# A broadcast row kept in PSUM, its biases added on ScalarE, and the split of the weights' low parts, in the opening stage of a hybrid layer

## The chip, the cores and the metric

The kernel runs on one core of a Trainium2 chip. The metric is the device time of one execution in microseconds (us). A core has five engines with queues of their own, each in order: PE (TensorE: matmuls and transposes, results into PSUM), DVE (VectorE), ACT (ScalarE), POOL (GpSimd) and SP (SyncE, which issues the DMAs here). Engines meet only at semaphores.

## The reference

One layer, a batch of 1, 256 tokens, width 2048, all in float32. Only the head of it concerns the change:

```python
shift, scale, gate = jnp.split(jax.nn.silu(c) @ w_ada + b_ada, 3, axis=-1)
h = rms_norm(x, norm_pre_w) * (1.0 + scale[:, None]) + shift[:, None]
proj = h @ w_in
```

`c` is one vector of 2048, `w_ada` is 2048 x 6144, `w_in` 2048 x 24,656. Two recurrent branches (a gated DeltaNet with 32 heads, an mLSTM with 8) use the columns of `proj`, and are merged with `sigmoid` gates that are columns of `proj` too; two projections, `w_out`, a second norm and the residual follow.

## The kernel before

**Precision.** Every float32 matmul with weights is made of three passes in the faster format fp32r. A matrix is split in a high part (ACT casts it, `whi`) and a low part (the matrix less the high part, `wlo`), on DVE or on POOL. `mm3` (lines 215 to 217) then issues high x high, high x low and low x high into one PSUM bank. `split_w` (line 176) decides for each half tile of 128x1024 where the low part is made: `share` counts up by `START_SHARE` for each half, and when it reaches one, POOL makes it. In the opening stage 0.625 of the halves go to POOL, later none.

**The opening stage** computes h and, as h comes into being, 14 groups of 512 columns of `w_in` that need no recurrence (the merge gates and the gates of three pairs of mLSTM heads). h needs shift and scale, so 32 MB of `w_ada` have to be read first; to keep PE at work the stage goes by blocks of k, chunks of 128 of the 2048 input channels: (0, 2), (2, 2), (4, 4), (8, 4), (12, 4) (first chunk, count). In each block all 14 groups are multiplied for the block's chunks. Groups 2 to 13 leave a partial sum in SBUF after each block: in the first ACT copies it (line 398), later DVE adds the bank to it (line 400). Groups 0 and 1 stay in four PSUM banks (`pr`, from the pool `pg`) throughout, with no copies or additions. Groups 2 to 13 take turns in the other four banks (`pn`, pool `pj`).

**Shift and scale** are not made on PE. `csil`, the row silu(c) repeated on all 128 partitions of SBUF, is made once by POOL (`partition_broadcast`, line 266). An ada tile is 128 output channels x 2048 inputs (1 MB); DVE multiplies it by `csil` and sums along the row in one instruction (line 331). Tile 2k gives shift of chunk k, tile 2k+1 its scale. Line 340 adds the bias to shift; line 315, in `h_chunk`, makes the factor of the norm from scale; ACT then computes the chunk of h (line 318) and casts it, and POOL makes its low part `h_lo`. `h_chunk(k)` is called straight behind the product of tile 2k+1.

**The head.** x is loaded, squared and summed (lines 276, 277), and POOL takes the root (`rsx`, line 213). ACT scales x with it (line 285), PE transposes it (line 291), ACT copies it back (line 293).

**Order.** `Stream` keeps a list of units (one weight tile or one ada tile), prepares each some three pieces ahead of its use, and loads a tile when its place in a ring of three is free (one ring for `w_in`, one for ada; the row `c` takes a place in the latter). All these loads are in SP's one queue in the list's order. `PACE` says how many ada tiles stand in the list before each block. `side` holds generators that advance by one step at each use: here, near the end of the stage, the gates' small work (lines 423 to 488) from the columns `pab`, which are multiplied between blocks 3 and 4. `branches_open` ends the stage: it drops the stage's SBUF and opens that of the recurrence.

Of the kernel before, what the change touches and what calls it, by code (L numbers as in the profile page):

```python
# [7 lines left out]
F32 = mybir.dt.float32  # L8
F32R = mybir.dt.float32r
AF = mybir.ActivationFunctionType  # L10
ALU = mybir.AluOpType
# [4 lines left out]
P = 128  # L16
# [5 lines left out]
QSCALE = 128.0 ** -0.5  # L22


START_SHARE = 0.625
STEP_US = 2.1
ROOM_US = 2.5

# [88 lines left out]
def hybrid_layer_kernel(  # L117
# [30 lines left out]
    hp = ctx.enter_context(tc.tile_pool(name="hp", bufs=1))  # L148
    yp = ctx.enter_context(tc.tile_pool(name="yp", bufs=2))
    pj = ctx.enter_context(tc.tile_pool(name="pj", bufs=4, space=PSUM))  # L150
    pg = ctx.enter_context(tc.tile_pool(name="pg", bufs=4, space=PSUM))
    dr = ctx.enter_context(tc.tile_pool(name="dr", bufs=1, space=DRAM))

    def const(name, src, shape):
# [38 lines left out]
    def gtile(nm, held=False):  # L193
        i = slots[0] % 4
        slots[0] += 1
        t = pg.tile([P, 512], F32, name=nm, tag="g")
        freed[i] = 1 << 30 if held else side.t + 1
        slots[1][id(t)] = i, t
        return t
# [9 lines left out]
    def jtile(nm):  # L209
        return pj.tile([P, 512], F32, name=nm, tag="pj")  # L210
# [13 lines left out]
    sil = cp.tile([P, KC], F32, name="sil")  # L224
    A.activation(sil, ct, AF.Silu)
    con = cp.tile([P, 512], F32, name="con")
    ident = con[:, 0:128]
    bd32 = con[:, 128:256]
    eunit = con[:, 256:512].rearrange("p (q i) -> p q i", q=8)
# [21 lines left out]
    rs = sp.tile([P, 2], F32, name="rsx")  # L251
    ad = sp.tile([P, 32], F32, name="ad")
    s1 = sp.tile([P, KC], F32, name="s1")
    part = [None, None] + [sp.tile([P, 2, 512], F32, name=f"part{g}") for g in range(2, len(START))]
    ADA_BUFS = 3

    csil = sp.tile([P, D], F32, name="csil")
    crow = sp.tile([P, D], F32, name="crow", tag="ar", bufs=ADA_BUFS)[0:1]
    SP.dma_start(crow, c_row)
    for b in range(2):  # L260
# [2 lines left out]
    bat = const("bat", b_ada_t, [P, 32])  # L263
    npre = const("npre", npre_t, [P, KC])
    A.activation(crow, crow, AF.Silu)
    G.partition_broadcast(csil, crow)
    late_c = {}

    def late_consts():
# [25 lines left out]
    def x_chunks(k0, k1):  # L295

        x_scale(k0)
        for k in range(k0, k1, 2):
            if k + 2 < k1:
                x_scale(k + 2)  # L300
            x_turn(k)
# [10 lines left out]

    def h_chunk(k):

        V.scalar_tensor_tensor(s1[:, k:k + 1], ad[:, KC + k:KC + k + 1], npre[:, k:k + 1], bnp[:, k:k + 1],
                               op0=ALU.mult, op1=ALU.add)
        hf = sp.tile([P, S], F32, name="hf", tag="hf", bufs=2)
        A.activation(hf.rearrange("p (b t) -> p b t", b=2), xs[:, :, k * P:(k + 1) * P], AF.Identity, bias=ad[:, k:k + 1], scale=s1[:, k:k + 1])
        split(hf, h_hi[:, k], h_lo[:, k], G)

    stream = Stream(load_w, side)
    BLOCKS = ((0, 2), (2, 2), (4, 4), (8, 4), (12, 4))
    PACE = (4, 9.5, 16.5, 25, 32, 32)

    def ada_units():

        adders = []
        for k in range(KC):
            for pt in range(2):
                def prep(h, raw, k=k, pt=pt):  # L330
                    V.scalar_tensor_tensor(raw, raw, 1.0, csil, op0=ALU.mult, op1=ALU.mult,  # L331
                                           accum_out=ad[:, pt * KC + k:pt * KC + k + 1])
                    if 4 <= 2 * k + pt < 8:
                        j = 2 * (2 * k + pt)
                        if j > 8:
                            x_turn(j)
                        if j < 14:
                            x_scale(j + 2)
                    if pt == 0:
                        V.tensor_tensor(ad[:, k:k + 1], ad[:, k:k + 1], bat[:, k:k + 1], op=ALU.add)  # L340
                    else:
                        h_chunk(k)
                        if k == 0:
                            x_chunks(6, 10)
                    return ()
                adders.append(lambda i=2 * k + pt, prep=prep:
                              stream.add(w_ada[i], prep, None, 1, load=(load_ada, "ada", ADA_BUFS)))
        return adders

    resident = {}  # L350
    br = ExitStack()

    def branches_open():

        nonlocal bp, x0, y0
        side.drain()
        share[:] = [0.0, 0.0]
        st.close()
        bp = br.enter_context(tc.tile_pool(name="bp", bufs=2))

        x0 = bp.tile([P, 8, P], F32, name="x0", tag="x0", bufs=1)
        y0 = bp.tile([64, 8, 64], F32, name="y0", tag="y0", bufs=1)
        G.memset(x0, 0.0)
        G.memset(y0, 0.0)

    def add_start_groups(bi):
        k0, nk = BLOCKS[bi]
        lastb = bi == len(BLOCKS) - 1
        adders, parts_ = [], []
        for g in range(len(START)):  # L370
            st_ = {}

            def use(h, hi, lo, g=g, st_=st_):
                if h == 0:
                    if g < 2:
                        if bi == 0:
                            resident[g] = [gtile(f"pr{i}") for i in range(2)]
                        st_["ps"] = resident[g]
                    else:
                        st_["ps"] = [jtile(f"pn{i}") for i in range(2)]  # L380
                for kc in range(min(2, nk - 2 * h)):
                    kr = h * 2 + kc
                    k = k0 + kr
                    o = kc * 512
                    for b in range(2):
                        mm3(st_["ps"][b], h_hi[:, k, b * P:(b + 1) * P], h_lo[:, k, b * P:(b + 1) * P],
                            hi[:, o:o + 512], lo[:, o:o + 512],
                            kr == 0 if g >= 2 else k == 0, kr == nk - 1 if g >= 2 else k == KC - 1)

            def after(g=g, st_=st_):  # L390
                if g < 2 and lastb:
                    part[g] = sp.tile([P, 2, 512], F32, name="res", tag="ar", bufs=ADA_BUFS)
                for b in range(2):
                    if g < 2:
                        if lastb:
                            A.activation(part[g][:, b], st_["ps"][b], AF.Sigmoid)
                    elif bi == 0:
                        A.copy(part[g][:, b], st_["ps"][b])
                    else:
                        V.tensor_tensor(part[g][:, b], st_["ps"][b], part[g][:, b], op=ALU.add)  # L400
                if bi == len(BLOCKS) - 2 and g == 3:
                    late_consts()
                if lastb:
                    if g >= 2:
                        pt = part[g].rearrange("p b c -> p (b c)")
                        A.activation(pt, pt, AF.Silu if g in (9, 11, 13) else AF.Sigmoid)
                    if g < 8:
                        SP.dma_start(gate_dr[g], part[g])
                    elif g % 2:
                        V.tensor_tensor(part[g], part[g], part[g - 1], op=ALU.mult)  # L410
                        SP.dma_start(gate_dr[8 + (g - 8) // 2], part[g])
                    if g == NG - 1:
                        branches_open()
            parts_.append((w_in[START[g]][:, k0 * 512:(k0 + nk) * 512], use, after))
        if nk == 2:
            for g in range(0, NG, 2):
                def use2(h, hi, lo, g=g):
                    parts_[g + h][1](0, hi, lo)
                    parts_[g + h][2]()
                adders.append(lambda g=g, use2=use2:  # L420
                              stream.add((parts_[g][0], parts_[g + 1][0]), prep_w, use2))
        else:
            for src, use, after in parts_:
                adders.append(lambda src=src, use=use, after=after:
                              stream.add(src, lambda h, raw: prep_w(h, raw, nk * 512), use, (nk + 1) // 2, after))
        return adders
# [63 lines left out]
    def add_ab():  # L490
        st_ = {}

        def use(h, hi, lo):
            if h == 0:
                st_["ps"] = jtile("pab")
            for j in range(8):
                k = h * 8 + j
                mm3(st_["ps"][:, 0:S], hi[:, j * P:(j + 1) * P], lo[:, j * P:(j + 1) * P], h_hi[:, k], h_lo[:, k],
                    k == 0, k == KC - 1)
        stream.add(w_ab, prep_w, use, after=lambda: side.add(gates(st_["ps"])))  # L500
# [4 lines left out]
    for bi, (k0, nk) in enumerate(BLOCKS):  # L505
        if bi == len(BLOCKS) - 1:
            add_ab()
        fs = add_start_groups(bi)
        for j, f in enumerate(fs):
            due = PACE[bi] + (PACE[bi + 1] - PACE[bi]) * j / len(fs)  # L510
            while ia < len(ada) and ia < due:
                ada[ia]()
                ia += 1
            f()
# [795 lines left out]
```

## Time and profile before

| | us |
|---|---|
| median of 3 runs | 1675.74 (1673.32 to 1677.84) |
| the profiled execution | 1673.93 |
| its span, first to last instruction | 1672.0 |
| busy in the span: PE, DVE, ACT, POOL | 1598.9, 1215.2, 923.4, 306.5 |
| busy from 26 to 300: PE, DVE, ACT, POOL | 249.6, 227.5, 123.3, 180.4 |
| mean granted clock of PE | 0.994 of full speed |
| moved by DMA | 372.4 MB, mean 223 GB/s |

A row of the timeline gives the start, the duration, the engine, the line, the operation, output <- inputs, shapes and a count, and in brackets how long the engine stood idle before it and what ended that. A row of the groups gives busy time and mean ns, then the idle time ahead. A row of the waits gives who waited for whom: total, times, longest. Matmuls overlap, so the duration of one (0.39 us) is longer than the distance from one to the next; PE's busy time is no measure of full pace.

### The profile page before, as it was taken

The page shows a single profiled execution, that of the slowest core. Times are in us where ns is not written, and L with a number is a line of the kernel's source. Part 1 is how long each engine was busy: PE and PEld are TensorE (multiplying, and loading weights), DVE is VectorE, ACT ScalarE, POOL GpSimd, SP SyncE. Part 2 cuts the span into 40 slices and gives each one's busy share as a digit, 9 for nine tenths or more (in the row PEclk, how much of TensorE's full clock was granted, in tenths as well). Part 3 has the DMA queues.
Part 4 walks back from the last instruction along what each step waited for, and adds up shares of the span by engine and source line. Part 5 has one row for each costly group of instructions (what it writes and reads, how often), then busy time and mean ns, then how long its engine had stood idle before and what let it go on. Part 6 is the DMA issues. An engine that isn't in the chain of part 4 may idle for free.

```text
span 1672.0 us, 25381 instructions
## 1 busy us (share of the span) xinstructions
PE 1598.9 (96%) x9836; PEld 1397.9 (84%) x9836; DVE 1215.2 (73%) x1799; ACT 923.4 (55%) x1462; POOL 306.5 (18%) x201
## 2 busy tenths in 40 slices
PE   3889999999999999999999999999999999999997
PEld 2767787778999898989898989889889788888886
DVE  5788888665677778787878787876778556756654
ACT  4733343755555657575757565755654644444443
POOL 2656766552000000000000000000010000100101
PEclk9989999999999999999999999999999999999999
DMA  9776776666555555555555555557888668766572
GB/s 348 283 276 252 301 282 231 227 239 227 183 187 170 179 164 186 183 178 171 173 176 183 166 168 178 178 164 248 282 285 307 251 248 292 276 243 237 210 269 109
DMA packets 96259, 372.37 MB, mean 223 GB/s; under 512 B 26261, under 2 KB 46213, under 8 KB 58249
## 3 DMA queue, kind: packets, MB, share of 16 engines
q1 hardware_dynamic: 96138, 370.75, 63.1%
q8 instruction: 77, 1.26, 0.3%
q14 instruction: 44, 0.36, 0.1%
HBM read 354.40 MB, written 16.31 MB: 222 GB/s over the span
## 4 chain that ended last, share of the span: by engine, by line
PE 64%; issue 15%; DVE 10%; ACT 5%; POOL 3%; DMA 2%; SPq 0%; DVEq 0%; ACTq 0%; POOLq 0%
PE pt L217 24%; PE pn L217 22%; PE py L217 8%; DVE wlo L169 3%; DVE ar L331 3%; ACT whi L168 2%; POOL wlo L169 2%; PE pr L217 1%; DVE part L400 1%; POOL mg L1118 1%; PE psa L217 1%; DVE gacc L1017 1%; DMA ya<-o_dr 1%; PE mq L761 1%; PE mz L769 1%
## 5 line engine op out<-in xcount | busy, mean ns | idle before, releaser
L169 DVE TENSOR_TENSOR wlo<-raw,whi 128x1024 fp32r<-128x1024 f32 x441 | 577.9, 1318 | 274.1 <-ACT whi L168 270.2
L168 ACT CAST whi<-raw 128x1024 fp32r<-128x1024 f32 x514 | 528.8, 1051 | 264.2 <-PE pn L217 92.6
L217 PE MATMUL pt<-h_hi,whi 128*128 128x256 f32 x1280 | 368.2, 288 | 0.0
L217 PE MATMUL pt<-h_hi,wlo 128*128 128x256 f32 x1280 | 362.6, 283 | 2.4 <-DVE wlo L169 1.5
L217 PE MATMUL pt<-h_lo,whi 128*128 128x256 f32 x1280 | 362.0, 283 | 0.0
L217 PE MATMUL pn<-whi,h_hi 128*128 128x512 f32 x832 | 331.2, 398 | 17.9 <-DVE part L400 9.4
L217 PE MATMUL pn<-wlo,h_hi 128*128 128x512 f32 x832 | 327.2, 393 | 4.9 <-POOL wlo L169 3.0
L217 PE MATMUL pn<-whi,h_lo 128*128 128x512 f32 x832 | 326.4, 392 | 0.0
L217 PEld LDWEIGHTS pt<-h_hi,wlo 128*128 128x128 f32 x1280 | 245.1, 191 | 3.5 <-DVE wlo L169 2.4
L217 PEld LDWEIGHTS pt<-h_hi,whi 128*128 128x128 f32 x1280 | 245.2, 192 | 1.4
L217 PEld LDWEIGHTS pt<-h_lo,whi 128*128 128x128 f32 x1280 | 245.3, 192 | 0.2
L169 POOL TENSOR_TENSOR wlo<-raw,whi 128x1024 fp32r<-128x1024 f32 x73 | 210.7, 2904 | 67.1 <-ACT whi L168 64.2
L217 PEld LDWEIGHTS pn<-whi,h_hi 128*128 128x128 f32 x832 | 157.7, 190 | 56.3 <-issue 9.8
L217 PEld LDWEIGHTS pn<-wlo,h_hi 128*128 128x128 f32 x832 | 157.7, 190 | 39.8 <-POOL wlo L169 5.5
L217 PEld LDWEIGHTS pn<-whi,h_lo 128*128 128x128 f32 x832 | 157.5, 189 | 33.5
L217 PE MATMUL py<-whi,yhi 128*128 128x512 f32 x384 | 150.6, 392 | 0.5 <-ACT vt L948 0.5
L217 PE MATMUL py<-whi,ylo 128*128 128x512 f32 x384 | 149.6, 389 | 0.0
L217 PE MATMUL py<-wlo,yhi 128*128 128x512 f32 x384 | 149.5, 389 | 0.0
L587 POOL TENSOR_SCALAR_AFFINE_SELECT dd<-gb 128x256 f32<-128x256 f32 x40 | 20.6, 538 | 441.4 <-DMA gb<-rows 341.0
L331 DVE SCALAR_TENSOR_TENSOR ar<-ar,csil 128x2048 f32<-128x2048 f32 x32 | 97.2, 3036 | 2.9 <-DMA ar<-in_dram 2.9
L168 ACT CAST yhi<-ya 128x512 fp32r<-128x512 f32 x48 | 29.9, 622 | 125.3 <-PE py L217 123.4
L169 DVE TENSOR_TENSOR ylo<-ya,yhi 128x512 fp32r<-128x512 f32 x48 | 33.2, 692 | 90.4 <-ACT yhi L168 88.5
(249 smaller groups left out, 2002.8 us busy)
## 6 DMA issues: line engine op xcount, KB each, us to landing
raw<-in_dram SPq DMA_DIRECT2D x259, 1024.0 KB
ar<-in_dram SPq DMA_DIRECT2D x32, 1024.0 KB
raw<-in_dram SPq DMA_DIRECT2D x28, 512.0 KB
ya<-o_dr SPq DMA_DIRECT2D x32, 256.0 KB
gb<-rows SPq DMA_DIRECT2D x20, 256.0 KB
gate_dr<-part SPq DMA_DIRECT2D x9, 512.0 KB
ug<-ud SPq DMA_DIRECT2D x32, 128.0 KB
o_dr<-oT SPq DMA_DIRECT2D x16, 256.0 KB
```

What stands on the lines that cost most here:

```text
L168: A.copy(hi, src)
L169: (eng or V).tensor_tensor(lo, src, hi.bitcast(F32), op=ALU.subtract)
L217: T.matmul(ps, l, r, start=start and i == 0, stop=stop and i == 2, skip_group_check=True)
L331: V.scalar_tensor_tensor(raw, raw, 1.0, csil, op0=ALU.mult, op1=ALU.mult, accum_out=ad[:, pt * KC + k:pt * KC + k + 1])
L400: V.tensor_tensor(part[g][:, b], st_["ps"][b], part[g][:, b], op=ALU.add)
L587: G.affine_select(dd[:, :, blk * S:blk * S + P], gb[:, :, blk * P:(blk + 1) * P], pattern=[[0, 2], [1, P]], compare_op=ALU.is_ge, fill=-1e ...
L761: T.matmul(psp[64:128, m * 64:(m + 1) * 64], um(m)[0:64, 64:128], y0[:, m], start=True, stop=True)
L769: T.matmul(psz[0:64, m * 64:(m + 1) * 64], p2[64:128, m], x0[64:128, m, 64:128], start=True, stop=True)
L1017: V.scalar_tensor_tensor(gate_half[q], raw[:, q * 1024:(q + 1) * 1024], sil[:, i:i + 1], gate_half[q], op0=ALU.mult, op1=ALU.add)
L1118: G.tensor_tensor(mcols(b, hf, cg), mcols(b, hf, cg), s_, op=ALU.add)
```

## The change

1. `csil` is made by four matmuls of a row of ones with the row silu(c) and stays in four PSUM banks until the end of the stage; `partition_broadcast` goes. The pool `pg` opens only then.
2. So groups 0 and 1 aren't resident any more: all 14 groups are copied or added to a partial sum, block by block.
3. The bias of shift and the factor from scale are made on ACT (`sh` and `s1`, 128x1 each) and no longer on DVE.
4. A chunk of h isn't queued straight behind its product but at the next chunk's first ada tile, or when a matmul needs it (`due`, `h_chunks`); chunk 0 at once.
5. `START_SHARE` is 0.8, and it falls to 0 with the last ada tile, not at the end of the stage. One number of `PACE` is 26 for 25.

```diff
-START_SHARE = 0.625
+START_SHARE = 0.8
...
-    pg = ctx.enter_context(tc.tile_pool(name="pg", bufs=4, space=PSUM))
+    pg = None
...
+    one_row = cp.tile([1, P], F32, name="one_row")
+    V.memset(one_row, 1.0)
...
-    part = [None, None] + [sp.tile([P, 2, 512], F32, name=f"part{g}") for g in range(2, len(START))]
+    sh = sp.tile([P, KC], F32, name="sh")
+    part = [sp.tile([P, 2, 512], F32, name=f"part{g}") for g in range(len(START))]
...
-    csil = sp.tile([P, D], F32, name="csil")
+    pcs = ExitStack()
+    csil = pcs.enter_context(tc.tile_pool(name="pcs", bufs=1, space=PSUM)).tile([P, D], F32, name="csil")
...
-    G.partition_broadcast(csil, crow)
+    for q in range(4):
+        T.matmul(csil[:, q * 512:(q + 1) * 512], one_row, crow[:, q * 512:(q + 1) * 512], start=True, stop=True)
...
     def h_chunk(k):
-        V.scalar_tensor_tensor(s1[:, k:k + 1], ad[:, KC + k:KC + k + 1], npre[:, k:k + 1], bnp[:, k:k + 1],
-                               op0=ALU.mult, op1=ALU.add)
+        A.activation(sh[:, k:k + 1], ad[:, k:k + 1], AF.Identity, bias=bat[:, k:k + 1])
+        A.activation(s1[:, k:k + 1], ad[:, KC + k:KC + k + 1], AF.Identity, bias=bnp[:, k:k + 1],
+                     scale=npre[:, k:k + 1])
...
-    PACE = (4, 9.5, 16.5, 25, 32, 32)
+    PACE = (4, 9.5, 16.5, 26, 32, 32)
+    due = []
+    def h_chunks(k):
+        while due and due[0] <= k:
+            h_chunk(due.pop(0))
...
-                    if pt == 0:
-                        V.tensor_tensor(ad[:, k:k + 1], ad[:, k:k + 1], bat[:, k:k + 1], op=ALU.add)
-                    else:
-                        h_chunk(k)
+                    h_chunks(k - 1)
+                    if pt == 1:
+                        due.append(k)
                         if k == 0:
+                            h_chunks(0)
                             x_chunks(6, 10)
+                        elif k == KC - 1:
+                            share[1] = 0.0
...
     def branches_open():
-        share[:] = [0.0, 0.0]
         st.close()
+        pcs.close()
+        pg = ctx.enter_context(tc.tile_pool(name="pg", bufs=4, space=PSUM))
...
-                    if g < 2:
-                        if bi == 0:
-                            resident[g] = [gtile(f"pr{i}") for i in range(2)]
-                        st_["ps"] = resident[g]
-                    else:
-                        st_["ps"] = [jtile(f"pn{i}") for i in range(2)]
+                    st_["ps"] = [jtile(f"pn{i}") for i in range(2)]
...
                     k = k0 + kr
+                    h_chunks(k)
...
-                    if g < 2:
-                        if lastb:
-                            A.activation(part[g][:, b], st_["ps"][b], AF.Sigmoid)
-                    elif bi == 0:
+                    if bi == 0:
                         A.copy(part[g][:, b], st_["ps"][b])
```

What moves, at three places. First POOL, from the program's start on (after its constants); `ISA` rows have no tile of their own. Before:

```order
L266 ISA
L266 ISA csil<-crow 128x2048
L213 ISA
L213 TENSOR_TENSOR rsx<-rsx,mhalf 128x2
L169 TENSOR_TENSOR h_lo<-hf,h_hi 128x256 x2
L169 TENSOR_TENSOR wlo<-raw,whi 128x1024 x2
L169 TENSOR_TENSOR h_lo<-hf,h_hi 128x256
```

And now:

```order
L213 ISA
L213 TENSOR_TENSOR rsx<-rsx,mhalf 128x2
L169 TENSOR_TENSOR h_lo<-hf,h_hi 128x256
L169 TENSOR_TENSOR wlo<-raw,whi 128x1024
L169 TENSOR_TENSOR h_lo<-hf,h_hi 128x256
L169 TENSOR_TENSOR wlo<-raw,whi 128x1024 x3
L169 TENSOR_TENSOR h_lo<-hf,h_hi 128x256
```

The broadcast is gone from ahead of the root, the second chunk's low part stands behind the first of the weights', and more low parts follow between two chunks.

Second ACT, from the transposed x (`xs`) to the first copies of partial sums. Before:

```order
L293 COPY xs<-xps 128x2x256 x2
L318 ACTIVATE hf<-xs,ad,s_103 128x256
L168 CAST h_hi<-hf 128x256
L285 ACTIVATE xs<-xs,rsx 128x256 x4
L293 COPY xs<-xps 128x2x256 x2
L318 ACTIVATE hf<-xs,ad,s_103 128x256
L168 CAST h_hi<-hf 128x256
L168 CAST whi<-raw 128x1024 x2
```

And now:

```order
L299 COPY xs<-xps 128x2x256 x2
L321 ACTIVATE sh<-ad,bat 128x1
L322 ACTIVATE s_102<-ad,bnp,npre 128x1
L325 ACTIVATE hf<-xs,sh,s_102 128x256
L168 CAST h_hi<-hf 128x256
L291 ACTIVATE xs<-xs,rsx 128x256 x4
L299 COPY xs<-xps 128x2x256 x2
L168 CAST whi<-raw 128x1024 x2
L291 ACTIVATE xs<-xs,rsx 128x256 x2
L321 ACTIVATE sh<-ad,bat 128x1
L322 ACTIVATE s_102<-ad,bnp,npre 128x1
L325 ACTIVATE hf<-xs,sh,s_102 128x256
```

The first two casts of weights have come ahead of the second chunk of h, and each chunk brings two operations of one column.

Third DVE, at the start of block 1 (`part_104` is the first partial sum that is kept: group 2 before, group 0 now). Before:

```order
L331 SCALAR_TENSOR_TENSOR ar,ad<-ar,csil 128x2048
L340 TENSOR_TENSOR ad<-ad,bat 128x1
L400 TENSOR_TENSOR part_105<-pn_668,part_105 128x512
L400 TENSOR_TENSOR part_105<-pn_669,part_105 128x512
L169 TENSOR_TENSOR wlo<-raw,whi 128x1024
L400 TENSOR_TENSOR part_106<-pn_691,part_106 128x512
L400 TENSOR_TENSOR part_106<-pn_692,part_106 128x512
L331 SCALAR_TENSOR_TENSOR ar,ad<-ar,csil 128x2048
L315 SCALAR_TENSOR_TENSOR s_103<-ad,npre,bnp 128x1
```

And now:

```order
L344 SCALAR_TENSOR_TENSOR ar,ad<-ar,csil 128x2048
L405 TENSOR_TENSOR part_105<-pn_635,part_105 128x512
L405 TENSOR_TENSOR part_105<-pn_636,part_105 128x512
L405 TENSOR_TENSOR part_106<-pn_658,part_106 128x512
L405 TENSOR_TENSOR part_106<-pn_659,part_106 128x512
L344 SCALAR_TENSOR_TENSOR ar,ad<-ar,csil 128x2048
L169 TENSOR_TENSOR wlo<-raw,whi 128x1024
L405 TENSOR_TENSOR part_107<-pn_687,part_107 128x512
```

The column operations behind each product are gone, and a low part of weights stands between the additions less often.

More of the change, by code (lines that the diff above doesn't have):

```diff
@@ L313, in h_chunk @@
     def h_chunk(k):
-        V.scalar_tensor_tensor(s1[:, k:k + 1], ad[:, KC + k:KC + k + 1], npre[:, k:k + 1], bnp[:, k:k + 1],
-                               op0=ALU.mult, op1=ALU.add)
+        A.activation(sh[:, k:k + 1], ad[:, k:k + 1], AF.Identity, bias=bat[:, k:k + 1])
+        A.activation(s1[:, k:k + 1], ad[:, KC + k:KC + k + 1], AF.Identity, bias=bnp[:, k:k + 1],
+                     scale=npre[:, k:k + 1])
         hf = sp.tile([P, S], F32, name="hf", tag="hf", bufs=2)
-        A.activation(hf.rearrange("p (b t) -> p b t", b=2), xs[:, :, k * P:(k + 1) * P], AF.Identity, bias=ad[:, k:k + 1], scale=s1[:, k:k + 1])
+        A.activation(hf.rearrange("p (b t) -> p b t", b=2), xs[:, :, k * P:(k + 1) * P], AF.Identity, bias=sh[:, k:k + 1], scale=s1[:, k:k + 1])
         split(hf, h_hi[:, k], h_lo[:, k], G)
@@ L348, in ada_units @@
         return adders
-    resident = {}
     br = ExitStack()
     def branches_open():
-        nonlocal bp, x0, y0
+        nonlocal bp, pg, x0, y0
         side.drain()
-        share[:] = [0.0, 0.0]
         st.close()
+        pcs.close()
+        pg = ctx.enter_context(tc.tile_pool(name="pg", bufs=4, space=PSUM))
         bp = br.enter_context(tc.tile_pool(name="bp", bufs=2))
@@ L386, in use @@
                         mm3(st_["ps"][b], h_hi[:, k, b * P:(b + 1) * P], h_lo[:, k, b * P:(b + 1) * P],
-                            hi[:, o:o + 512], lo[:, o:o + 512],
-                            kr == 0 if g >= 2 else k == 0, kr == nk - 1 if g >= 2 else k == KC - 1)
+                            hi[:, o:o + 512], lo[:, o:o + 512], kr == 0, kr == nk - 1)
             def after(g=g, st_=st_):
-                if g < 2 and lastb:
-                    part[g] = sp.tile([P, 2, 512], F32, name="res", tag="ar", bufs=ADA_BUFS)
                 for b in range(2):
-                    if g < 2:
-                        if lastb:
-                            A.activation(part[g][:, b], st_["ps"][b], AF.Sigmoid)
-                    elif bi == 0:
+                    if bi == 0:
                         A.copy(part[g][:, b], st_["ps"][b])
@@ L403, in after @@
                 if lastb:
-                    if g >= 2:
-                        pt = part[g].rearrange("p b c -> p (b c)")
-                        A.activation(pt, pt, AF.Silu if g in (9, 11, 13) else AF.Sigmoid)
+                    pt = part[g].rearrange("p b c -> p (b c)")
+                    A.activation(pt, pt, AF.Silu if g in (9, 11, 13) else AF.Sigmoid)
                     if g < 8:
@@ L497, in use @@
                 k = h * 8 + j
+                h_chunks(k)
                 mm3(st_["ps"][:, 0:S], hi[:, j * P:(j + 1) * P], lo[:, j * P:(j + 1) * P], h_hi[:, k], h_lo[:, k],
@@ L509, in hybrid_layer_kernel @@
         for j, f in enumerate(fs):
-            due = PACE[bi] + (PACE[bi + 1] - PACE[bi]) * j / len(fs)
-            while ia < len(ada) and ia < due:
+            ahead = PACE[bi] + (PACE[bi + 1] - PACE[bi]) * j / len(fs)
+            while ia < len(ada) and ia < ahead:
                 ada[ia]()
```

## The prediction, written before the run

> **What bounds the kernel now.** I read the chain of waits first, then the busy times of one stretch, then who PE waited for in it. The times (us from the span's start) say where the opening stage lies:
>
> ```profile
> 31.54 1.22 DVE wlo L169
> ...
> 227.01 27.21 PE pn L217 x120
> ...
> 295.76 5.75 PE pab L217 x48
> ...
> 384.81 0.39 PE L217 MATMUL pn<-whi,h_lo 128*128 128x512 f32 x1
> ```
>
> The first weight matmul follows the low part of 31.54 (it starts at 31.57); the gate columns `pab` start at 295.76, when k blocks 0 to 3 are through; the last `pn` of the opening stage is at 384.81. 120 matmuls in 27.21 us are 0.2268 us each at full pace. Blocks 0 to 3 hold 14 groups x 12 k x 2 halves of the rows x 3 = 1008 matmuls, 228.6 us at that pace, and take 264.2: **35.6 us lost**. Block 4 holds 336 (76.2 us) and `pab` 5.75; 295.76 to 385.04 is 89.3: **7.3 lost**. And 31.57 us pass before the first. Behind 385 the change alters nothing, so everything hangs on these three sums. What ends PE's waits, from 26 to 296 us:
>
> ```profile
> PE pn L217 <- DVE part L400: 9.4, 5, 3.6
> PE pn L217 <- ACT part L398: 4.2, 3, 2.0
> PE pn L217 <- ACT whi L168: 4.2, 4, 1.2
> PE pr L217 <- ACT whi L168: 2.6, 1, 2.6
> PE xps L291 <- ACT xs L285: 2.1, 1, 2.1
> PE pr L217 <- POOL wlo L169: 1.4, 2, 1.1
> PE pn L217 <- POOL wlo L169: 1.1, 2, 0.7
> PE pr L217 <- DVE wlo L169: 0.5, 1, 0.5
> ```
>
> The largest is an addition on DVE. Why DVE is late stands in its groups for the same stretch (count, then busy us and mean ns), and in single rows:
>
> ```profile
> L331 DVE SCALAR_TENSOR_TENSOR ar<-ar,csil 128x2048 f32<-128x2048 f32 x28 | 88.0, 3142 | 0.0
> L169 DVE TENSOR_TENSOR wlo<-raw,whi 128x1024 fp32r<-128x1024 f32 x33 | 67.7, 2052 | 40.4 <-ACT whi L168 40.3
> L400 DVE TENSOR_TENSOR part<-pn,part 128x512 f32<-128x512 f32 x72 | 45.8, 680 | 3.4 <-PE pn L217 3.3
> L340 DVE TENSOR_TENSOR ad<-ad,bat 128x1 f32<-128x1 f32 x14 | 25.8, 1839 | 0.5
> L315 DVE SCALAR_TENSOR_TENSOR s<-ad,npre,bnp 128x1 f32<-128x1 f32 x14 | 5.1, 363 | 0.5
> ...
> 39.36 1.21 DVE L169 TENSOR_TENSOR wlo<-raw,whi 128x1024 fp32r<-128x1024 f32 x1
> 40.50 2.28 DVE L331 SCALAR_TENSOR_TENSOR ar<-ar,csil 128x2048 f32<-128x2048 f32 x1
> ...
> L400 DVE TENSOR_TENSOR part<-pn,part x68: 672/680/692, 100.9 to 295.8; 128x512 f32<-128x512 f32 x68
> ...
> L169 POOL TENSOR_TENSOR wlo<-raw,whi x55: 2361/2500/4507, 32.5 to 297.2; 128x1024 fp32r<-128x1024 f32 x55
> L169 POOL TENSOR_TENSOR h_lo<-hf,h_hi x16: 729/748/2848, 26.6 to 287.2; 128x256 fp32r<-128x256 f32 x16
> ```
>
> An addition of one column takes 1.8 us on average: it isn't working, it is waiting for something that a running GpSimd instruction holds. The product `ar<-ar,csil` takes 2.28 alone and 3.14 on average, DVE's low part 1.21 and 2.05. But `part<-pn,part`, which reads one operand from PSUM, is 672 to 692 ns in all 68 cases, beside whatever GpSimd does. So DVE with two SBUF operands and GpSimd exclude each other. Sum of the work that takes turns, each at its undisturbed time: 28 x 2.28 + 33 x 1.21 + 14 x 0.16 + 14 x 0.22 (the small ones) + 55 x 2.36 + 16 x 0.73 = 251 us of 270. This shared path, 93% taken, bounds blocks 0 to 3.
>
> **The product.** Its second operand moves to PSUM. If it then leaves the shared path as line 400 does, the sum becomes (64 low parts on GpSimd before `pab` and 25 on DVE, counted in the order of the changed kernel) 64 x 2.36 + 16 x 0.73 + 25 x 1.21 = 193 us. The trace shows no 2048-wide DVE operation from PSUM: at least 28 x 2.28 is the present price of one, and four rows of line 400 (2.72 us) bound it above; I take 2.3, nearest to the row of equal width. The Trainium skill (SBUF — State Buffer, "Who interferes with whom") says that a DVE instruction with at most one SBUF input, outside the two-port modes, doesn't contend with GpSimd, and that the loser of a conflict blocks wholly. The trace agrees for line 400; for a product that writes SBUF and reads SBUF first no run here shows it, and if the rule doesn't reach it the second rival below is what happens.
>
> **Biases and chunk order.** The 28 small operations leave DVE: 30.9 us there. On ACT they are 32 of about 0.2 us (the 32x1 row below), 6 us on an engine busy 116 of 264. A chunk of h is now queued one ada tile later.
>
> ```profile
> 304.44 0.19 ACT L443 ACTIVATE na<-alog 32x1 f32<-32x1 f32 x1
> ACT hf L318 <- DVE s L315: 86.3, 14, 11.1
> 31.50:295.80 264.30, 243.41 (x1022) 194.72 (x1023) 226.45 (x188) 116.09 (x148) 175.10 (x68) 0.97 0.72 273
> 60.00:100.00 40.00, 34.13 (x146) 27.35 (x147) 31.42 (x25) 23.24 (x35) 25.82 (x10) 0.98 0.91 349
> 140.00:180.00 40.00, 38.28 (x165) 30.71 (x166) 33.79 (x28) 15.76 (x18) 29.77 (x12) 1.00 0.76 293
> ```
>
> ACT stood 86 us in front of those chunks with casts queued behind; most of that goes. (In the windows: PE, PEld, DVE, ACT, POOL busy, clock, DMA share, GB/s.)
>
> **No resident groups.** 12 more additions x 0.64 (45.8/72) = 8 us on DVE, 4 more copies x 0.6 on ACT. DVE in all: 28 x 2.3 + 25 x 2.05 + 84 x 0.64 = 169 us against 226 now, so they lie in its new idle time; without it they would cost their 8.
>
> **Blocks 0 to 3.** Of the 35.6, the waits behind 31.57 are 20.8 (the eight rows without the 2.6 and the 2.1, which end before it). Clock 0.97 costs 264 x 0.03 = 8, the rest is small gaps and transposes. I take away the 9.4 (additions), the 4.2 (casts) and half of the clock's 8, add 0.7 for the copies (4.2 x 14/12) and leave the low parts' 3.0, though more of them come from GpSimd: about **17 us**. Nothing gained at all, or everything but the first warm-up (30), are the bounds.
>
> **Start.**
>
> ```profile
> 2.77 1.91 ACT L265 ACTIVATE crow<-crow 1x2048 f32<-1x2048 f32 x1
> 11.33 0.17 DVE L280 TENSOR_SCALAR rsx<-rsx 128x2 f32<-128x2 f32 x1
> 12.59 2.29 DVE L331 SCALAR_TENSOR_TENSOR ar<-ar,csil 128x2048 f32<-128x2048 f32 x1 [1.00 <-DMA ar<-in_dram]
> 15.30 0.90 SPq L163 DMA_DIRECT2D raw<-in_dram  x2
> 20.22 0.73 POOL L213 TENSOR_TENSOR rsx<-rsx,mhalf 128x2 f32<-128x2 f32 x1 [10.13 <-DVE ar L331]
> 20.98 1.71 ACT L285 ACTIVATE xs<-xs,rsx 128x256 f32<-128x256 f32 x4 [10.65 <-POOL rsx L213]
> 22.06 2.29 DVE L331 SCALAR_TENSOR_TENSOR ar<-ar,csil 128x2048 f32<-128x2048 f32 x1 [1.64 <-DMA ar<-in_dram]
> 1296.44 1.02 PE L1028 MATMUL gps<-gacc,ones 128*1 128x512 f32 x2
> ```
>
> The norm's root waits on GpSimd from 11.50 to 20.22, behind the broadcast, another piece of code for it (an "ISA" row in the order), and three products. Broadcast and products leave its way, so it runs at about 11.6. From there ACT needed 30.57 - 20.98 = 9.6 us to the first cast; one chunk (1.0) moves behind it, two small operations (0.4) come in: 9.0, so the cast starts near 21.3 and the first matmul follows near 22.5, or 23 if `raw`, issued at 15.30, lands late. The second k then waits for the fourth product (24.35, set by the DMA), 1.4 us of ACT and 0.7 of GpSimd, about 0.9 behind the first six matmuls. Gain **8 us**. The four matmuls for `csil` are each like the two rows of line 1028 (0.95 us to the next matmul), 3.8 us, 7.6 at half clock; from 4.68 they end at 12.3 at worst, ahead of the first `ar` at 12.59. If they begin only when the broadcast does now (7.79), products and loads slip 3 us: bounds 5 and 9.
>
> **Last block.** Low parts now all on DVE, whose sum is 28 x 1.21 + 28 x 0.64 and the gates' work (under 20), about 70 of 82 us.
>
> ```profile
> PE tp L484 <- DVE part L400: 2.3, 1, 2.3
> PE pn L217 <- POOL wlo L169: 2.0, 3, 1.1
> ```
>
> These two waits (296 to 389 us) are ones that GpSimd makes, directly or by holding DVE: **4 us**, bounds 0 and 7.
>
> **Sum:** 8 + 17 + 4 = 29 on 1673.93, the profiled execution's own time (span 1672.0 plus 1.9 around it; the median of the three runs, 1675.74, is 1.8 above): **1645 us**.
>
> **Rivals.** *Transfers bound it.* The same bytes in 264 - 17 = 247 us need 292 GB/s; the row of 60 to 100 shows 349 at a share of 0.91, so there is room, but loads wait in one queue for three-deep rings, and 140 to 180, where little holds PE up, shows 293 and not more. Held at 282, between that and today's 273, the phase takes 264 x 273/282 = 256: 9 instead of 17, **1653**. *The product still takes the shared path,* the change not doing what it says: path sum 193 + 64 = 257 at 93% is no better than now, the root still waits; the small operations' 31 us and the 4 of the last block stay: some 6 + 4, **1664**. *GpSimd becomes the bound,* on the other side:
>
> ```profile
> POOL h_lo L169 <- ACT h_hi L168: 76.7, 16, 9.5
> 46.60 0.60 PE L217 MATMUL pn<-whi,h_hi 128*128 128x512 f32 x1 [2.01 <-ACT part L398]
> 47.00 0.63 PE L217 MATMUL pn<-wlo,h_hi 128*128 128x512 f32 x1
> ```
>
> Four of five low parts queue on GpSimd behind its h_lo, which waited 76.7 us. With 193 us of turns, its slack in 247 is 54; should the chunks still hold it 77, it needs 270, PE idles 41, and after each of 16 gaps runs at 0.4 us and more a matmul instead of 0.23 for eight matmuls, as after the 2.01 us gap above (0.2 x 8 x 16 = 26): phase 296, +32 - 8 - 4 = +20, **1694**. It decides from 54 us of such waits, 3.4 per chunk. Against it: the chunk is queued a whole tile behind its product, and PE waited only 2.5 us for GpSimd so far. The Trainium skill (TensorE: Matmul & The Clock Gate, Part 1) lets the clock fall after an idle window of some 3.4 us; by it gaps of 2.6 us would not cool PE and this rival would give about 1668. The 2.01 us gap did, so the measurement decides.
>
> **Chances.** Forecast 62% (own range 1632 to 1656), transfers 15%, shared path 10%, GpSimd 7%, nothing that shows 6%. A measurement tells about 0.3% (5 us) from no change. Faster by more: 62 + 15 + most of the third, 0.86; within 0.07; slower 0.07. The range goes from start 9 + 30 + 4 below (1631) to the second rival (1664).
>
> **What would show it.** Products all near 2.3 us beside running GpSimd; the root near 12 and the first weight matmul near 23 us; `pab` near 270 and the last `pn` near 352; no wait of ACT for `ad` above some us; GpSimd idle behind `pab`. Wrong if products still stretch to 3 or 4.5, if the root stays at 20, or if PE's waits for GpSimd's low parts or for `ar` and `raw` grow to tens of us.

## The result, and the profile after

| | before | after |
|---|---|---|
| median of the runs, us | 1675.82 | 1634.48 (1634.28 to 1636.31) |
| profiled execution: time / span, us | 1673.93 / 1672.0 | 1634.3 / 1632.5 |
| first weight matmul, us from the span's start | 31.57 | 24.27 |
| `pab` follows k blocks 0 to 3 | 295.76 | 257.88 |
| end of the opening stage's last `pn` | 385.04 | 348.67 |
| first `gps` | 1296.44 | 1257.01 |

The ratio of the times is 0.9756, interval 0.974 to 0.9773: faster by 41 us, where 29 were forecast. The difference of the spans is 39.5 us. By the stations of the table the opening gained 7.3 us ahead of the first weight matmul and 30.6 in blocks 0 to 3 (264.2 to 233.6), and gave back 1.5 in the last block (89.3 to 90.8). The other 3.1 come behind the opening.

The chain of waits after, cut to the parts that answer to those of before (start us, us, what):

```profile
10.87 0.70 POOL rsx L213
...
11.99 7.43 DMA ar<-in_dram
...
22.14 11.00 DMA raw<-in_dram
...
43.39 214.49 PE pn L217 x945
257.88 2.77 PE pab L217 x23
...
260.67 1.05 ACT whi L168
261.72 0.20 ACT sh L321
...
262.22 0.61 ACT hf L325
...
263.34 0.74 POOL h_lo L169
...
264.12 0.40 PE pab L217
```

From 43.39 on 945 matmuls follow each other in one piece, 214.49 us, 0.227 us each: the full pace of the prediction's first fence. Until `pab` the chain doesn't leave PE again. The next idle time of PE is inside `pab` itself, where chunk 15 of h (cast, shift, `hf`, `h_lo`) is late.

What ended PE's waits, 20 to 360 us, after (us in total, times, longest):

```profile
PE tp L488 <- DVE part L405: 3.6, 1, 3.6
PE pn L217 <- ACT whi L168: 3.4, 1, 3.4
PE pn L217 <- DVE wlo L169: 2.1, 2, 1.7
PE pab L217 <- POOL h_lo L169: 0.4, 1, 0.4
PE pn L217 <- ACT part L403: 0.2, 1, 0.2
```

The 3.4 is the one that ends with the first weight matmul, and 1.7 of the 2.1 lies in the last block. In blocks 0 to 3, 0.6 us of waits are left of 20.8. DVE's groups after, 20 to 260 us (count, then busy us and mean ns, then the idle time before them and its releaser):

```profile
L344 DVE SCALAR_TENSOR_TENSOR ar<-ar,csil 128x2048 f32<-128x2048 f32 x30 | 68.4, 2280 | 12.3 <-DMA ar<-in_dram 12.3
L405 DVE TENSOR_TENSOR part<-pn,part 128x512 f32<-128x512 f32 x84 | 56.0, 688 | 48.0 <-PE pn L217 48.0
L169 DVE TENSOR_TENSOR wlo<-raw,whi 128x1024 fp32r<-128x1024 f32 x24 | 30.9, 1287 | 30.9 <-ACT whi L168 30.9
```

The product's own line after (ns min/median/max, first and last start):

```profile
L344 DVE SCALAR_TENSOR_TENSOR ar<-ar,csil x32: 2271/2278/2289, 12.3 to 236.8; 128x2048 f32<-128x2048 f32 x32
```

Windows after (us; busy us of PE, PEld, DVE, ACT, POOL with counts; granted clock, DMA share, GB/s):

```profile
24.27:257.88 233.61, 232.99 (x1022) 191.66 (x1023) 145.31 (x163) 128.62 (x179) 163.43 (x78) 1.00 0.85 325
257.88:348.67 90.79, 85.04 (x390) 70.36 (x390) 58.84 (x76) 62.94 (x69) 1.74 (x5) 0.98 0.62 225
20.00:60.00 40.00, 36.02 (x153) 28.25 (x152) 22.10 (x19) 34.84 (x61) 26.60 (x14) 1.00 1.01 409
```

All 32 products take 2271 to 2289 ns, though GpSimd works 163 of the 233.6 us: the mean of 3142 before has become the undisturbed time. Additions on DVE now wait for PE (48.0 us) and not PE for them. DMA moved 325 GB/s over the phase, and 409 in the window of 20 to 60. The same turn-round shows in ACT's waits, 20 to 360 us:

```profile
ACT whi L168 <- PE pn L217: 98.6, 61, 1.7
```

and in GpSimd's, same stretch:

```profile
POOL h_lo L169 <- ACT h_hi L168: 36.4, 7, 23.7
```

ACT's casts wait 98.6 us for PE to free their buffers, and no row of 86 us for DVE's column operation is left. PE bounds blocks 0 to 3.

### The profile page after: what moved, and what is told of

Read it like the earlier page. It is cut to its first block, busy times and chain, and to the rows that moved or that the text cites. A ratio compares the mean times of both kernels' runs of the same rounds, so it can differ in the third digit from the quotient of the medians.

```text
span 1632.5 us, 25436 instructions
## 1 busy us (share of the span) xinstructions
PE 1595.8 (98%) x9844; PEld 1398.7 (86%) x9844; DVE 1137.3 (70%) x1793; ACT 937.5 (57%) x1496; POOL 241.7 (15%) x191
## 4 chain that ended last, share of the span: by engine, by line
PE 78%; issue 13%; DVE 3%; ACT 2%; DMA 2%; POOL 1%; SPq 0%; DVEq 0%; POOLq 0%; ACTq 0%
PE pn L217 34%; PE pt L217 27%; PE py L217 8%; DVE wlo L169 1%; ACT whi L168 1%; POOL mg L1123 1%; PE psa L217 1%; DMA raw<-in_dram 1%; PE mq L766 1%; PE mz L774 1%; PE mp L741 1%; PE pt L848 0%; DMA ar<-in_dram 0%; PE po L811 0%; PE pc L801 0%
## 5 line engine op out<-in xcount | busy, mean ns | idle before, releaser
L169 DVE TENSOR_TENSOR wlo<-raw,whi 128x1024 fp32r<-128x1024 f32 x450 | 552.7, 1237 | 273.3 <-ACT whi L168 272.4
L217 PE MATMUL pn<-whi,h_hi 128*128 128x512 f32 x896 | 354.3, 395 | 3.5 <-ACT whi L168 3.4
L217 PE MATMUL pn<-wlo,h_hi 128*128 128x512 f32 x896 | 350.5, 391 | 3.0 <-DVE wlo L169 3.0
L217 PE MATMUL pn<-whi,h_lo 128*128 128x512 f32 x896 | 350.4, 391 | 0.0
L217 PEld LDWEIGHTS pn<-whi,h_hi 128*128 128x128 f32 x896 | 169.1, 189 | 40.1 <-ACT whi L168 3.8
L217 PEld LDWEIGHTS pn<-wlo,h_hi 128*128 128x128 f32 x896 | 169.2, 189 | 38.4 <-DVE wlo L169 4.3
L217 PEld LDWEIGHTS pn<-whi,h_lo 128*128 128x128 f32 x896 | 169.0, 189 | 35.8 <-POOL h_lo L169 0.3
L169 POOL TENSOR_TENSOR wlo<-raw,whi 128x1024 fp32r<-128x1024 f32 x64 | 153.6, 2408 | 44.2 <-ACT whi L168 44.2
L405 DVE TENSOR_TENSOR part<-pn,part 128x512 f32<-128x512 f32 x112 | 74.0, 687 | 48.0 <-PE pn L217 48.0
L567 DVE SCALAR_TENSOR_TENSOR qs<-pt,gcv,qs 128x255 f32<-128x255 f32 (+2 forms) x192 | 92.2, 480 | 4.6
```

Of the source, the lines that this page charges most:

```text
L169: (eng or V).tensor_tensor(lo, src, hi.bitcast(F32), op=ALU.subtract)
L217: T.matmul(ps, l, r, start=start and i == 0, stop=stop and i == 2, skip_group_check=True)
L567: V.scalar_tensor_tensor(dst[:, n, sh:], src[:, 0:S - sh], taps(n, 3 - sh), dst[:, n, sh:], op0=ALU.mult, op1=ALU.add)
```

## The experiments

Each ratio is to the kernel before on the same chip, with its interval; the kernel after has 0.9756. Stations in us, each the start of the first matmul of its kind in one profiled execution (the chain above counts `pab` 0.2 us later): weights, `pab`, `psa` (just behind the opening) and `gps`; phase is `pab` less weights.

| kernel | ratio | weights | pab | phase | psa | gps |
|---|---|---|---|---|---|---|
| before | 1 | 31.57 | 295.6 | 264.0 | 439.6 | 1296.4 |
| after | 0.9756 (0.974 to 0.9773) | 24.27 | 257.7 | 233.4 | 402.0 | 1257.0 |
| e1_self | 0.9841 (0.9821 to 0.9861) | 24.57 | 275.1 | 250.5 | 419.2 | 1274.7 |
| e2_bcast | 0.9788 (0.9762 to 0.9815) | 31.27 | 264.0 | 232.7 | 408.3 | 1263.0 |
| e3_dvebias | 0.981 (0.9793 to 0.9826) | 24.45 | 268.0 | 243.6 | 415.7 | 1271.3 |
| e4_soon | 0.9767 (0.975 to 0.9783) | 26.66 | 262.8 | 236.1 | 405.9 | 1260.4 |
| e5_dvebias_soon | 0.9768 (0.9747 to 0.9788) | 26.31 | 262.5 | 236.2 | 406.8 | 1261.7 |
| e6_share625 | 0.9756 (0.9734 to 0.9778) | 23.77 | 257.5 | 233.7 | 401.7 | 1256.6 |
| e7_sharetail | 0.975 (0.9731 to 0.9769) | 24.24 | 257.7 | 233.5 | 401.2 | 1257.2 |
| e8_last | 0.9747 (0.9726 to 0.9767) | 24.27 | 258.2 | 233.9 | 401.4 | 1257.0 |
| e9_last_tp | 0.974 (0.9717 to 0.9763) | 23.02 | 256.9 | 233.9 | 398.6 | 1256.9 |
| e11_others | 0.9883 (0.9861 to 0.9905) | 31.96 | 281.9 | 249.9 | 423.7 | 1278.7 |
| e12_notable | 0.9736 (0.9716 to 0.9757) | 24.37 | 258.3 | 233.9 | 401.2 | 1256.4 |

### The product's second operand back in SBUF (e1_self)

```diff
-                    V.scalar_tensor_tensor(raw, raw, 1.0, csil, op0=ALU.mult, op1=ALU.mult,
+                    V.scalar_tensor_tensor(raw, raw, 1.0, raw, op0=ALU.mult, op1=ALU.mult,
```

> The product of an ada tile reads the tile twice from SBUF instead of the tile and the row in PSUM (shift and scale are then not the reference's); everything else as in the changed kernel. Port theory (two SBUF operands exclude GpSimd, and this alone filled blocks 0 to 3): products stretch from 2.28 to about 3 us on average, work that takes turns is 193 + 64 = 257 us, so from the first matmul to pab some 255 to 262 us instead of 233.6, and the time is 1655 to 1663 us. Rival, order theory (what went was ACT standing in front of the chunks of h, 86 us before): products may stretch, but the phase stays near 234 to 240 and the time within 5 us of 1634.5.

Everything else of the change stays; `csil` is still made by matmuls, so the head is the same. DVE's groups, 20 to 260 us:

```profile
L344 DVE SCALAR_TENSOR_TENSOR ar<-ar 128x2048 f32<-128x2048 f32 x30 | 103.7, 3461 | 6.1 <-DMA ar<-in_dram 6.1
L405 DVE TENSOR_TENSOR part<-pn,part 128x512 f32<-128x512 f32 x76 | 49.4, 681 | 19.2 <-PE pn L217 19.2
L169 DVE TENSOR_TENSOR wlo<-raw,whi 128x1024 fp32r<-128x1024 f32 x17 | 44.0, 2587 | 24.9 <-ACT whi L168 24.9
```

Products are stretched to 3461 ns again, low parts to 2587 (1287 after), while the additions with an operand in PSUM stay at 681. The phase loses 17.1 us, the time 14 by the ratios (0.0085 x 1676). A phase of 250.5 is short of the 255 to 262 expected by the port theory, and farther from its rival's 234 to 240. The operand's place is what stretches the product. The Trainium skill (SBUF — State Buffer, "Who interferes with whom") says that only the port pair which DVE's second SBUF operand shares with GpSimd is contended for; the two runs agree for this instruction too, 2280 against 3461 ns.

### Everything but the product and its room (e11_others)

The kernel before with the biases on ACT, the later chunk and the larger share for GpSimd; `csil` is broadcast into SBUF and the two resident groups stay. The edit is the change's diff without its parts on `csil` and on `pr`.

> The kernel before with only the other edits: column operations on ACT, chunks one tile late, share 0.8 that falls to 0; broadcast row in SBUF, groups 0 and 1 resident. The root should stay at 20 us and the first matmul near 31. If the gain of these edits doesn't need the product from PSUM (e1_self kept 13 of 30 us in blocks 0 to 3 without it): phase 248 to 254 instead of 264, time 10 to 16 us under the kernel before. If more low parts on GpSimd on a path that is still shared eat it: within 4 us of the kernel before, or slower.

Its phase is 249.9 us, as expected; the time falls by 20 us (0.0117 x 1676), more than the 10 to 16 expected. 14.1 of the 30.6 come without the product's move, with products at 3500 ns. e1_self, the same but for the resident groups and the head, has 250.5; so giving up the resident groups shows no price. The parts can't be added each by itself: these alone bring 14.1, the product on top of them 17.1, but the product without the column operations and the later chunk brings 27.8 (e5, below).

### The broadcast back, its result unused by the product (e2_bcast)

```diff
+    for q in range(2):
+        G.partition_broadcast(part[q].rearrange("p b c -> p (b c)"), crow[:, q * 1024:(q + 1) * 1024])
```

> Changed kernel with two broadcasts of half the row each by GpSimd ahead of the root of the norm, into tiles that are overwritten later; the product still uses PSUM. If the root was held before by the pieces of code that GpSimd changes between broadcast and root: root at 17 to 21 us, first weight matmul at 30 to 32 as before the change, time 1640 to 1643. If it was held by the three products on the shared path: these don't take it now, so the root runs right behind the broadcasts, at 11 to 13 us, and the time stays at 1634 to 1637.

The prediction put the root's wait down to two things, the change of code on GpSimd and the three products ahead of it; here the first is back and the second isn't. GpSimd's timeline, 5 to 24 us (start us, us, what, in brackets the idle time before):

```profile
7.56 2.61 POOL L274 PARTITION_BROADCAST part<-crow  x2 [7.12 <-issue]
20.25 0.73 POOL L213 TENSOR_TENSOR rsx<-rsx,mhalf 128x2 f32<-128x2 f32 x1 [10.08 <-issue]
```

The root runs at 20.25, as in the kernel before (20.22), with no product on the shared path, and GpSimd idle for 10.08 us in which it waits for nothing that the profile shows. DVE wrote its operand from 11.41 to 11.58, so 8.7 us of it are lost. So the broadcast holds the root up without the products, and the profile of before, which named `DVE ar L331` as the releaser, named what happened to end last. That it does so by the change of code is argued from idle time for which the profile has no cause; no run has the one without the other. The first weight matmul comes 7.0 us later, the time is 5 longer (0.0032 x 1676). The Trainium skill (GPSIMD Engine Reference, "2.1 Instruction dispatch") counts approximately 6 us, with no instruction in the profile, for the first call of a freshly loaded kernel; here the idle time is 10.08 us by the records.

### Biases back on DVE (e3), the chunk at once (e4), both (e5)

```diff
-        A.activation(sh[:, k:k + 1], ad[:, k:k + 1], AF.Identity, bias=bat[:, k:k + 1])
-        A.activation(s1[:, k:k + 1], ad[:, KC + k:KC + k + 1], AF.Identity, bias=bnp[:, k:k + 1],
-                     scale=npre[:, k:k + 1])
+        V.tensor_tensor(sh[:, k:k + 1], ad[:, k:k + 1], bat[:, k:k + 1], op=ALU.add)
+        V.scalar_tensor_tensor(s1[:, k:k + 1], ad[:, KC + k:KC + k + 1], npre[:, k:k + 1], bnp[:, k:k + 1],
+                               op0=ALU.mult, op1=ALU.add)
```

> Changed kernel, but the two column operations of each chunk are made on DVE again (still one tile late). Port theory: each waits for GpSimd's running instruction, some 1.2 to 1.8 us, 40 to 55 us in all on DVE, which has 88 us idle in the phase: time 1634 to 1640. Order theory: no change beyond noise, since the chunk's place in ACT's queue is the same. A third reading, that these 31 us of DVE were themselves the bound: 1650 or more.

```diff
                     if pt == 1:
                         due.append(k)
+                        h_chunks(k)
                         if k == 0:
-                            h_chunks(0)
```

> Changed kernel, but a chunk of h is queued on ACT straight behind its product again. Port theory: with products that no longer stretch, ACT stands for them a shorter time and the casts are far enough ahead: 1632 to 1640. Order theory: ACT's wait for the product comes back (50 us and more of 86) and PE waits for casts: 1645 to 1665. The last chunk is ready earlier in this form, so 3 us of the wait at pab may go.

e5_dvebias_soon has both edits.

> Changed kernel with the column operations on DVE and each chunk straight behind its product, so that of the change the product from PSUM, the missing residency and the share are left. If the parts add up (9 us for the one, 2 to 3 for the other, 14 for the product): 1645 to 1649. If the two are one cost seen twice (ACT waiting for DVE's column operations): 1643 to 1646. If the product's path carried everything else: 1636 to 1640.

One row of ACT's waits, 20 to 360 us (total, times, longest), from each; first e3:

```profile
ACT hf L325 <- DVE s L322: 50.5, 15, 7.7
```

e4:

```profile
ACT s L322 <- DVE ar L344: 39.3, 12, 6.5
```

e5:

```profile
ACT hf L325 <- DVE s L322: 52.6, 14, 6.7
```

e3 misses its expectation: 10 us more in the phase and 9 by the ratios, 14 by the spans of the profiled executions. e4 and e5 lose 2 by the ratios, whose intervals overlap with that of the kernel after, and 3.5 and 4.6 by the spans, 2.4 and 2.0 of it ahead of the first weight matmul; e5's phase, 236.2, still is 27.8 below that of before. ACT stands in front of its chunks for 39 to 53 us in all three, so that sum doesn't price them. What sets e3 apart is when the chunk comes: its column operations are queued on DVE a tile late, behind the next product, so the chunk that waits for them is late by both. PE's waits for `h_hi` in e3 (2.5 and 1.0 us, none in e5) agree. All of PE's waits behind the first weight matmul come to 7.1 us in e3's phase against 0.6 in that of the kernel after; that the chunk's lateness explains all of the 10 is argued, not shown. So the late chunk needs the biases on ACT (with biases on DVE it costs 10 us), but not the other way round: e4 has the biases on ACT without it and loses little. Where the product reads PSUM, it alone (with the share and the resident groups' room) carries 27.8 of the 30.6.

### GpSimd's share as before (e6), and kept in the last block (e7)

```diff
-START_SHARE = 0.8
+START_SHARE = 0.625
```

> Changed kernel with START_SHARE 0.625 again. Port theory: turns are about 50 x 2.36 + 39 x 1.21 + 12 = 177 us of 234, DVE gets 15 low parts more (18 us and their waits), both have room: within 3 us of 1634.5. If the share of 0.8 was itself part of the gain (DVE would be late with additions): 1640 to 1650.

```diff
-                        elif k == KC - 1:
-                            share[1] = 0.0
...
     def branches_open():
+        share[:] = [0.0, 0.0]
```

> Changed kernel, but GpSimd goes on making four of five low parts to the end of the opening stage. The prediction's term for the last block (4 us for low parts on DVE alone) would show here with its sign turned: 3 to 5 us slower. If the last block is held by ACT's casts and table loads instead, who makes the low parts is nothing: within 2 us, with 1.3 us lost at most behind the stage's end.

Neither differs from the kernel after. Who makes the low parts is nothing once PE is the bound; in the last block too, where e7's wait of `tp` is 2.1 us and its waits for additions and GpSimd's low parts 2.3 more.

### The last chunk and the gates (e8, e9, e12)

e8 queues chunk 15 straight behind its product; e9 also puts the gates' transposes into the bank that `csil` has left; e12 leaves the sigmoid of the eight merge gates out (Identity in its place), and with it six of the nine loads of a function table that ACT makes from 265 to 295 us.

```diff
                         elif k == KC - 1:
                             share[1] = 0.0
+                            h_chunks(k)
...
-        tp = jtile("tp")
+        tp = csil[:, 0:512]
```

```diff
-                    A.activation(pt, pt, AF.Silu if g in (9, 11, 13) else AF.Sigmoid)
+                    A.activation(pt, pt, AF.Silu if g in (9, 11, 13) else AF.Sigmoid if g >= 8 else AF.Identity)
```

> Changed kernel, but chunk 15 is queued on ACT straight behind its product, since no later ada tile calls for it. If the 3.4 us that PE waits at pab for a cast are due to chunk 15 being called only by the matmul that needs it: that wait and the 0.4 for its low part go, with the slower clock behind them, 4 to 6 us: 1628 to 1631. If the cast is late for another reason (the table loads of the gates): no change.

> The kernel with chunk 15 early, and the transposes of the gates' rows go to the PSUM of the row instead of a bank that waits for DVE's additions. If PE's 3.6 us there are a wait for the bank: they go, 1624 to 1628. If they are a wait for the gates' last exponential on ACT: no change against the kernel with chunk 15 early, 1628 to 1631.

> Changed kernel without the sigmoid of the eight merge gates (they are stored as they are), so that ACT needs no other table for them between the gates' exponentials and logarithms. If casts behind table loads are what PE lacks from 265 to 295 us: PE's busy time there rises from 24.7 to 27 us or more, and the first psa comes 3 to 5 us earlier. If the transposes' bank alone is the loss: no change there, under 1 us.

The chain of e8, where PE goes through `pab` without a stop, and where it takes up the groups behind the gates:

```profile
258.36 5.65 PE pab L217 x47
264.03 1.05 ACT whi L168
...
294.20 0.45 PE tp L489
...
295.29 4.75 PE pn L217 x16
```

After, the piece behind the gates starts at 295.35: the 3 us that `pab` gains are given back at once, because the next cast of weights starts at 264.03 here and at 264.55 there, and the gates' work on ACT and DVE behind it takes the same 31 us. That misses the expectation. e9 takes the wait of `tp` away, as expected, and is 3.4 us ahead at `psa` (0.8 of it at `pab` already), but at `gps` it stands at 1256.9 against 1257.0, and its ratio isn't told from that of the kernel after: the time expected, 1624 to 1628, is missed. The 3.4 us were lost between the last `psa` (1013.7 against 1017.1) and `gps`, in a stretch which the edit doesn't touch. Two rows of PE and a window of e9 show where:

```profile
1044.18 0.59 PE L753 MATMUL mx<-pcm,xcmp 32*32 32x32 f32 x13 [0.93 <-ACT pcm L744]
1046.10 0.63 PE L217 MATMUL pn<-wlo,h_hi 128*128 128x512 f32 x1
1042.60:1052.50 9.90, 8.98 (x85) 7.00 (x85) 3.68 (x3) 6.23 (x12) 0.00 (x0) 0.83 0.59 146
```

PE waits 0.93 us there for an operation of ACT, which it doesn't in the kernel after; behind the `mx` matmuls the clock reads 0.83 and eight weight matmuls follow each other at some 0.43 us instead of 0.23. Together that is 2.6 of the 3.4 us. Why ACT was late at this place is open.

In e12 PE is busy 25.95 of the 30 us from 265 on, against 24.72 after, where 27 or more were expected if the loads were the cause, and `psa` comes 0.8 us earlier instead of 3 to 5. So these six loads are a small part of what the gates cost.

## Why the prediction was right, and where its sum was off

**Bound.** Right for the most part. DVE with two SBUF operands and GpSimd took turns, and most of the bound went with the operand (e1_self, e5_dvebias_soon): these two engines meet at this path too, and not only at semaphores. But the path didn't bound all four blocks alike, as the windows by block below show.

**Start, 8 forecast, 7.3 measured.** The root at 10.86 ("near 12"), the first weight matmul at 24.27 ("near 23"). Its cast waited 1.59 us for `raw`, the late landing that the prediction allowed for. Of the causes that it named for the root's wait, the broadcast with its code does it without the products (e2_bcast). The head's 7 us are worth 6.3 at `pab`.

**Blocks 0 to 3, 17 forecast, 30.6 measured.** This term was mis-sized, and with it the sum. The prediction took away 9.4 (additions), 4.2 (casts) and 4 of the clock's 8, and added 0.7. It kept PE's waits for copies (4.2 + 0.7), for low parts (3.0), and most of the 14.8 that stood behind no wait. Afterwards 5.0 us are lost in the phase in place of 35.6: waits of 20.8 have become 0.6, and the clock reads 1.00 in place of 0.97. In us that is 20.2 less of waits, where 12.9 were taken away (9.4 + 4.2 - 0.7), and 10.4 less of the rest, where 4 were. The prediction gave each wait its own cause, the casts to the chunks and the low parts to GpSimd. But e5_dvebias_soon, where ACT still stands 52.6 us in front of the chunks, gains 27.8 in the phase: nearly all these waits, whichever engine their rows name, hung on the one shared path, and the phase came out at the prediction's own upper bound, everything but the warm-up (30). That the clock and the small gaps went because the waits went is argued, not tried by itself.

Windows of one block each could have told more (columns as above; 168, 168, 336 and 336 matmuls with weights). Before, then PE's largest wait in block 1 (80.80 to 133.40):

```profile
31.57:80.80 49.23, 44.53 (x180) 35.02 (x181) 38.09 (x27) 33.27 (x53) 31.82 (x13) 0.97 0.82 301
80.80:133.40 52.60, 43.57 (x170) 34.13 (x169) 46.50 (x47) 17.30 (x22) 29.30 (x12) 0.90 0.71 265
133.40:215.90 82.50, 77.82 (x337) 62.58 (x336) 71.34 (x59) 32.08 (x36) 59.68 (x22) 1.00 0.72 278
215.90:295.60 79.70, 77.29 (x338) 62.78 (x337) 70.30 (x57) 33.37 (x37) 54.10 (x22) 1.00 0.68 257
PE pn L217 <- DVE part L400: 8.2, 4, 3.6
```

After:

```profile
24.27:67.30 43.03, 42.41 (x180) 33.84 (x181) 21.72 (x18) 38.58 (x67) 31.12 (x16) 1.00 1.01 406
67.30:105.30 38.00, 38.00 (x169) 31.47 (x168) 33.88 (x43) 20.65 (x29) 31.29 (x16) 1.00 0.97 383
105.30:181.50 76.20, 76.20 (x338) 63.10 (x337) 46.92 (x55) 36.91 (x48) 57.25 (x28) 1.00 0.84 318
181.50:257.70 76.20, 76.20 (x337) 63.09 (x337) 42.61 (x50) 32.48 (x36) 43.78 (x20) 1.00 0.71 259
```

The gain is 6.2, 14.6, 6.3 and 3.5 us. Nearly half of it lies in block 1, where `PACE` puts 7 ada tiles beside 168 matmuls, and where 8.2 of the 9.4 us of waits for additions and the low clock, 0.90, stand together. In block 3, 7 tiles go with 336 matmuls; DVE and GpSimd are about as busy there as in block 2, and yet PE loses only 3.5 of 79.7 us. There the path was full but hardly held PE up, so a sum of busy times over all the blocks didn't show where the bound lay.

**Last block, 4 forecast, -1.5 measured.** This term was wrong in its cause. It said that GpSimd makes the waits for `tp` and for low parts; e7_sharetail, with GpSimd in the last block as before, stands where the kernel after does. The waits moved (`tp` 2.3 to 3.6) and one is new, chunk 15 in `pab`. Taking these two away brings 3.4 us at `psa`, 0.8 of it there at `pab` already (e9_last_tp), and nothing that shows in the time. What else holds the gates' 30 us is not settled.

**Behind the opening, 0 forecast, 3.1 measured.** The prediction had it that the change alters nothing there. 1.3 of it is at `psa`: GpSimd's low parts ran on past the end of the opening in the kernel before, and PE waited for one; now there are none. GpSimd's timeline of before from 381 us on:

```profile
386.72 4.74 POOL L169 TENSOR_TENSOR wlo<-raw,whi 128x1024 fp32r<-128x1024 f32 x2 [4.38 <-ACT whi L168]
```

And PE's waits of before, 385 to 1300 us:

```profile
PE mpt L931 <- DVE hn L958: 1.0, 3, 0.4
PE pt L217 <- POOL wlo L169: 0.8, 1, 0.8
PE mx L747 <- ACT pcm L738: 0.3, 1, 0.3
```

The other 1.8 lies between `psa` and `gps`. 1.3 of it are the waits for `hn` and `pcm`, which the kernel after doesn't have; the change touches neither operation, and e9_last_tp lost 3.4 in this stretch, 2.6 of them by one such wait and the clock behind it. So no gain of the change is shown there.

**Small parts.** Biases and the later chunk took DVE's column operations and ACT's 86 us away, as foreseen, but with the product in PSUM they are worth some 2 to 5 us together at most (e5, not told from nothing by the ratios), 14 with the share where the product is still in SBUF (e11). The larger share is worth nothing (e6). The 26 for 25 in `PACE` was not tried by itself.

**The number.** It fell inside the stated range, but the sum is partly luck: the blocks were held 13.6 us too low and the last block 5.5 too high. Of the signs, `pab` came at 257.88 ("near 270"). The last `pn` ended at 348.67 ("near 352"), but that 352 doesn't follow from the sum, which gives 385 - 29 = 356.

**Rivals.** Transfers as the bound fell: 325 GB/s against the 282 at which that rival held them. The product on the shared path fell with its 2271 to 2289 ns. GpSimd as the bound fell: its `h_lo` waited 36.4 us, 23.7 of them for chunk 15 alone, and PE waited 0.4 us for GpSimd.

## What to carry to other kernels

An operation whose mean is far above its shortest time, or a tiny one as long as a neighbour's instruction, may be waiting for a path that two engines share: where it is DVE with two SBUF operands beside GpSimd, try one operand in PSUM before moving the work. When one path feeds all the late engines, size its removal by the full pace of PE, block by block, and not by the waits that name it. A call that is put off needs someone who makes it in time for the last item as well (here that cost 3 us at `pab`, and nothing in the time).

## What the runs showed of the hardware

- GpSimd stood idle for 10.08 us between a broadcast and the root, 8.7 of them with the root's operand ready, and no row tells of it (e2_bcast); ahead of the broadcast it was 7.12. A change of code is the likely reason, not a shown one.
- Behind a wait of PE of 0.93 us and 1.4 us of 32x32 matmuls came eight weight matmuls at 0.43 us each (e9_last_tp, granted clock 0.83); behind the same 32x32 matmuls without a wait ahead of them (the kernel after) the clock reads 1.00.
- DMA reached 409 GB/s over 40 us at a share of 1.01, while PE, DVE, ACT and GpSimd worked.
- A product of a tile with itself is stretched by GpSimd too (3461 ns, e1_self): it is the count of SBUF operands that matters, not of tiles.
- A column operation on ACT took 0.28 to 0.39 us in the head, against the 0.2 of a 32x1 row; two rows of the timeline after:

```profile
16.10 0.30 ACT L321 ACTIVATE sh<-ad,bat 128x1 f32<-128x1 f32 x1
17.02 0.39 ACT L322 ACTIVATE s<-ad,bnp,npre 128x1 f32<-128x1 f32 x1 [0.63 <-DVE ar L344]
```
